# One-operation one-hot tables, a later choice for the fourth tile, and two-tile fronts in the first half of a decoder-layer kernel

## The chip, the cores and the metric

The kernel runs on one core of a Trainium2 chip. The metric is the device time of one execution in microseconds (us); less is better. The kernel before took 3437.81 us, the median of three runs (3435.53 to 3441.62). Its engines are TensorE (PE, with its weight loads as PEld), VectorE (DVE), ScalarE (ACT), GpSimd (POOL), which here issues the gathers, and SyncE (SP), which issues the other transfers.

## The reference

One decoder layer over 1024 tokens of width 1024, in float32. First a mixer (a gated short convolution and three groups of dilated attention, merged by sigmoid gates), then an expert layer:

```
s  = q . sub_keys                       # per token: 8 heads x 2 halves x 128 scores
top 16 of each half; top 16 of the 16x16 sums -> idx (of 16384 experts), gates = softmax
a  = gelu(x . expert_down[idx])         # 128 experts per token
h += sum_e gates_e * a_e * expert_up[idx_e]
out = rms_norm(h, final_norm)
```

## The kernel before

The tokens are worked on in two halves of 512, each of four tiles of 128 tokens. `mixer(0)` runs for the first half, then `mixer(1)` for the second. Every product with float32 weights is split: `weights` (L161) loads 512 KB, ScalarE rounds it to `hi` (L165), VectorE subtracts to get `lo` (L167), and `mm3` (L175 to L178) makes three matmuls per piece of 128 rows.

At the end of a mixer stand, for a *front* of tiles, the 16 gate projections (`gates`, L604), the merge (`merge`, L616: 8 projections of half depth with `w_attn_out`, 8 with `w_conv_out`), and for a *sub* of a front the output product (`product`, L663) and the `tail` (L694: norm, turn, 16 query projections of which the scores are stored). `SUBS` (L42) gives fronts and subs per half: `((1, 2), (1, 1))`, that is one front of four tiles with two subs of two tiles in the first half, and one of each in the second. While a tail waits at its start, `AFTER` = 4 steps of what comes next are put ahead of it.

The expert layer is done in two ways.

- **First half, by gathers** (`experts`, L872). For each of the four tiles `choose` (L756, VectorE alone, 16 rounds of top-8 operations and a decoding) gives 128 expert numbers per token. Each is a gather of 512 KB issued on POOL's queue into one of four row buffers: a *down* (L885 with the VectorE operation L887) or an *up* (L908 with L910). The steps are in the order of `STEPS` (L49): downs of tiles 0, 1, 2; ups of tile 0, which TensorE sums (`summed`, L930); ups of tiles 1 and 2; downs and ups of tile 3. Tile 0 is chosen during its own tail, tiles 1 to 3 in `mixer(1)` at the places that `CHOOSE = (0, 1, 2, 3)` (L47) gives: tile 3 during the second half's merge, and what is left of it at the start of `chosen(0)` (L1001).
- **Second half, densely** (`dense`, L971). TensorE multiplies all 16384 experts' down rows with the tokens (`hidden`, L985, 128 projections). The gates of the chosen experts become a dense table. `build` (L1011) makes for four tokens at a time (a *group*; 128 groups in all) two one-hot tables `oa` and `ob`, `ob` with the gate in it; TensorE multiplies them; ScalarE copies the product (`psg`) from PSUM into `stg`, which goes to memory (`g_d`) chunk by chunk, eight groups to a chunk. Then `weigh` (L1046) reads the whole table back expert by expert and multiplies, and TensorE applies the up rows.

`hidden` for the first ten blocks of four projections is interleaved with the four choices and builds of the second half and with `summed`; this is called the *hidden stretch* below. The first `weigh` needs every chunk of the table; from there on the kernel is in its *last stage*.

Before, `ob` is made in one of two ways: in every other group ScalarE takes four operations of 128 columns (L1029) and one of 512 (L1030) and VectorE one of 512 (L1031); in the others VectorE takes one of 512 (L1033) and ScalarE four of 128 (L1036). The copies are four of 128 columns (L1040).

A scheduler orders each engine's instructions when the program is built, from the order in which the code emits them (paced by `RATE_G` and the `PACE` constants) and from when buffers come free. The engines then run them in that fixed order.

## Time and profile before

| | us |
|---|---|
| median of three runs | 3437.81 |
| the profiled execution | 3448.45 |
| its span, first to last instruction | 3446.7 |
| TensorE busy | 3165.5 (92%) |
| VectorE busy | 2669.4 (77%) |
| ScalarE busy | 1398.0 (41%) |
| POOL busy | 1422.7 (41%) |

The profiled execution lies 10.6 us above the median of the runs. Times below are from the span's start. The stages: attention and gates of the first half until 650, its tails until about 790; `mixer(1)` until about 1500; its tail until 1620; the hidden stretch and the build until 2176; the last stage from 2198 on. A matmul's listed duration is longer than what it occupies, since matmuls are pipelined, and so, less strongly, is an operation's on VectorE and ScalarE: the time from one start to the next is the better measure where an engine doesn't wait.

### The profile page before, as it was taken

Reading aid. Unit: us, or ns where it says so; the run is one execution under the profiler, and the core shown is the slowest. Engines: PE = TensorE matmul, PEld = TensorE weight load, DVE = VectorE, ACT = ScalarE, POOL = GpSimd, SP = SyncE. Lnnn points to the kernel's source line nnn. Section 1 sums busy time; section 2 is a strip of 40 time slices with the busy share of each in tenths; the row PEclk is TensorE's granted clock in tenths of the full one; section 3 lists DMA queues with packets and bytes.
Section 4 is the critical chain, followed back from the end, with each engine's and each line's share of the span. In section 5 each row is a group of like instructions: output and inputs, shape, how many; then the busy total and the mean of one; then the engine's idle time right before and its main releaser. Section 6 shows DMA issues by size and latency. Waiting matters only on the chain.

```text
span 3446.7 us, 45451 instructions
## 1 busy us (share of the span) xinstructions
PE 3165.5 (92%) x15410; PEld 2559.9 (74%) x15410; DVE 2669.4 (77%) x5357; ACT 1398.0 (41%) x2898; POOL 1422.7 (41%) x1101
## 2 busy tenths in 40 slices
PE   7999999999899997979779985699999999999996
PEld 6788788887677875768556764588887878778775
DVE  5333455799999989888987748888887878778887
ACT  3544444543344362333465678332322232222222
POOL 0000000024555455555555334455555656555555
PEclk9999999999999997989889997799999999999998
DMA  4233345778888888999888887999999999999997
GB/s 131 77 118 115 95 136 201 237 251 308 295 297 306 306 304 276 344 321 338 307 295 328 322 316 280 335 341 329 324 347 327 333 330 329 327 322 336 322 318 276
DMA packets 349225, 965.26 MB, mean 280 GB/s; under 512 B 35264, under 2 KB 118720, under 8 KB 346432
## 3 DMA queue, kind: packets, MB, share of 16 engines
q0 software_dynamic: 152064, 551.62, 44.6%
q1 hardware_dynamic: 196928, 410.74, 35.0%
q8 instruction: 121, 1.98, 0.2%
q14 instruction: 112, 0.92, 0.1%
HBM read 885.61 MB, written 70.32 MB: 277 GB/s over the span
## 4 chain that ended last, share of the span: by engine, by line
PE 29%; DMA 16%; issue 14%; DVE 12%; POOL 9%; ACT 2%; SPq 1%; POOLq 0%; DVEq 0%; ACTq 0%
DMA rowu<-in_up,idx 7%; POOL row L885 6%; PE ps L178 5%; PE ps L176 5%; PE ps L177 5%; DMA row<-in_down,idx 4%; DVE row L887 4%; POOL rowu L908 3%; PE held L176 2%; PE held L177 2%; PE held L178 2%; PE psg L1038 2%; DVE lo L167 1%; PE upacc L944 1%; DVE acc L910 1%
## 5 line engine op out<-in xcount | busy, mean ns | idle before, releaser
L885 POOL DMA_INDIRECT row<-in_down,idx x512 | 668.9, 1306 | 670.9 <-DVE a L887 331.2
L908 POOL DMA_INDIRECT rowu<-in_up,idx x384 | 559.1, 1456 | 456.9 <-DVE acc L910 392.8
L165 ACT CAST hi<-raw 128x1024 fp32r<-128x1024 f32 x368 | 387.0, 1052 | 788.3 <-PE ps L177 491.7
L887 DVE CUSTOM_DVE_ANT_0 row<-row,ut 128x1024 f32<-128x1024 f32 x512 | 618.1, 1216 | 94.9 <-DMA row<-in_down,idx 89.3
L167 DVE TENSOR_TENSOR lo<-raw,hi 128x1024 fp32r<-128x1024 f32 x368 | 449.0, 1220 | 259.7 <-ACT hi L165 246.8
L910 DVE SCALAR_TENSOR_TENSOR acc<-rowu,a,acc 128x1024 f32<-128x1024 f32 x384 | 492.4, 1282 | 141.6 <-DMA rowu<-in_up,idx 132.1
L178 PE MATMUL ps<-vhi,lo 128*128 128x512 f32 (+1 forms) x1408 | 531.4, 377 | 29.1 <-DVE lo L167 27.4
L176 PE MATMUL ps<-vhi,hi 128*128 128x512 f32 (+1 forms) x1408 | 527.3, 375 | 5.8 <-ACT ga L989 3.6
L177 PE MATMUL ps<-vlo,hi 128*128 128x512 f32 (+1 forms) x1408 | 526.7, 374 | 0.1
L176 PE MATMUL ps<-uhi,hi 128*128 128x512 f32 x1024 | 407.0, 399 | 7.8 <-ACT hi L165 5.3
L178 PE MATMUL ps<-uhi,lo 128*128 128x512 f32 x1024 | 407.7, 399 | 2.0 <-DVE lo L167 1.9
L177 PE MATMUL ps<-ulo,hi 128*128 128x512 f32 x1024 | 406.7, 397 | 0.5 <-DVE ulo L182 0.5
L178 PEld LDWEIGHTS ps<-vhi,lo 128*128 128x128 f32 x1408 | 267.9, 190 | 84.5 <-DVE lo L167 34.7
L176 PE MATMUL held<-uh,hh 128*128 128x512 f32 x752 | 290.2, 395 | 24.9 <-ACT hh L181 24.9
L176 PEld LDWEIGHTS ps<-vhi,hi 128*128 128x128 f32 x1408 | 268.0, 190 | 54.8 <-ACT ga L989 5.3
L177 PEld LDWEIGHTS ps<-vlo,hi 128*128 128x128 f32 x1408 | 268.1, 190 | 46.7 <-issue 1.2
L177 PE MATMUL held<-ul,hh 128*128 128x512 f32 x752 | 297.1, 395 | 5.3 <-DVE ul L182 5.3
L178 PE MATMUL held<-uh,hl 128*128 128x512 f32 x752 | 294.9, 393 | 0.0
L181 ACT CAST uh<-rawu 128x1024 fp32r<-128x1024 f32 x126 | 131.6, 1049 | 380.6 <-DMA rawu<-in_up_s 310.8
L932 POOL DMA_DIRECT2D acc<-h_d x1 | 0.7, 691 | 619.1 <-DMA h_d<-h 619.1
L176 PEld LDWEIGHTS ps<-uhi,hi 128*128 128x128 f32 x1024 | 193.3, 189 | 54.5 <-ACT hi L165 7.8
L1038 PE MATMUL psg<-oa,ob 128*128 128x128 f32 x1024 | 157.9, 316 | 80.0 <-ACT stg L1040 42.7
(336 smaller groups left out, 5581.2 us busy)
## 6 DMA issues: line engine op xcount, KB each, us to landing
raw<-in_w_proj SPq DMA_DIRECT2D x128, 512.0 KB
raw<-in_down_t SPq DMA_DIRECT2D x128, 512.0 KB
rawu<-in_up_s SPq DMA_DIRECT2D x128, 512.0 KB
g_d<-stg SPq DMA_DIRECT2D x64, 512.0 KB
gg<-g_d SPq DMA_DIRECT2D x32, 1024.0 KB
raw<-in_w_query SPq DMA_DIRECT2D x48, 512.0 KB
raw<-in_w_v SPq DMA_DIRECT2D x24, 512.0 KB
raw<-in_w_out SPq DMA_DIRECT2D x24, 512.0 KB
```

The lines of the kernel that those rows point to most:

```text
L165: S.copy(hi, raw)
L167: V.tensor_tensor(lo, raw, hi.bitcast(F32), op=ALU.subtract)
L176: PE.matmul(ps, l[0], r[0], start=first, stop=False)
L177: PE.matmul(ps, l[0], r[1], start=False, stop=False)
L178: PE.matmul(ps, l[1], r[0], start=False, stop=last)
L181: S.copy(hi, src)
L885: G.indirect_dma_start(out=row, out_offset=None, in_=down, in_offset=bass.IndirectOffsetOnAxis(ap=idx[:, e:e + 1], axis=0))
L887: V.tensor_tensor_reduce(out=row, in0=row, in1=ut, scale=1.0, scalar=0.0, op0=ALU.mult, op1=ALU.add, accum_out=a[:, e:e + 1])
L908: G.indirect_dma_start(out=row, out_offset=None, in_=up, in_offset=bass.IndirectOffsetOnAxis(ap=idx[:, e:e + 1], axis=0))
L910: V.scalar_tensor_tensor(acc, row, a[:, e:e + 1], acc, op0=ALU.mult, op1=ALU.add)
L944: m = PE.matmul(part[n][32 * j:32 * j + 32], z[:, j, c0:c0 + 32], rows[j][:, n * TH:n * TH + TH], start=s == 0, stop=s == 31)
L1038: PE.matmul(ps[:, t], ob[:, t], oa[:, t], start=True, stop=True)
```

## The change

- The one-hot table `ob` is made by VectorE alone, four operations of 128 columns that compare and multiply in one; ScalarE has no part in it. The copies are two of 256 columns in place of four of 128, and the stores two of 1 MB per chunk in place of four of 512 KB. `OBUF` goes from 4 to 3 and `STG` from 5 buffers of 4 KB per partition to 3 of 8 KB.
- The choice for tile 3 of the first half is no longer advanced in `mixer(1)` and not finished in `chosen(0)`; it is emitted with the ups of tile 2, a step after every fourth up, once the builds have been emitted.
- `SUBS` is `((2, 1), (1, 1))`: the first half has two fronts of two tiles, each with its gates, merge, product and tail. Gate and merge weights are loaded and split twice, and their matmuls have 256 columns in place of 512. The first tile is chosen in the first front's tail.

```
-SUBS = ((1, 2), (1, 1))
-OBUF = 4
+SUBS = ((2, 1), (1, 1))
+OBUF = 3
-CHOOSE = (0, 1, 2, 3)
+CHOOSE = (0, 1, 2, 0)
-STG = 5
+STG = 3
...
                     V.scalar_tensor_tensor(acc, row, a[:, e:e + 1], acc, op0=ALU.mult, op1=ALU.add)
+                    if tt == 2 and e % 4 == 3:
+                        while "built" not in place:
+                            yield 1.0
+                        next(later[3], None)
                     yield 1.0
...
         def chosen(tt):
-            if tt == 0:
-                yield from later[ORDER[3]]
...
-                    stg = [den.tile([P, 32, TC], F32, tag="stg", bufs=STG, name="stg") for _ in range(4)]
+                    stg = [den.tile([P, 64, TC], F32, tag="stg", bufs=STG, name="stg") for _ in range(2)]
...
-                        if t4 % 2 == 0:
-                            for t in range(4):
-                                S.activation(ob[:, t], iota, AF.Abs, bias=i2[:, t:t + 1], scale=-1.0)
-                            S.activation(ob, ob, AF.Relu, bias=ones[:, 0:1], scale=-1.0)
-                            V.tensor_tensor(ob, ob, gv[:, :, None].to_broadcast([P, 4, P]), op=ALU.mult)
-                        else:
-                            V.tensor_tensor(ob, iota[:, None, :].to_broadcast([P, 4, P]),
-                                            i2[:, :, None].to_broadcast([P, 4, P]), op=ALU.is_equal)
-                            for t in range(4):
-                                S.mul(ob[:, t], ob[:, t], gv[:, t:t + 1])
+                        for t in range(4):
+                            V.tensor_scalar(ob[:, t], iota, i2[:, t:t + 1], gv[:, t:t + 1], op0=ALU.is_equal, op1=ALU.mult)
...
-                        for w in range(4):
+                        for w in range(2):
                             S.copy(stg[w][:, :, t4 * 4:t4 * 4 + 4],
-                                   ps[:, :, 32 * w:32 * w + 32].rearrange("p t i -> p i t"))
+                                   ps[:, :, 64 * w:64 * w + 64].rearrange("p t i -> p i t"))
...
         for _ in builder:
             yield 0.0
+        place["built"] = True
```

Three places in the order of the instructions. In the kernel after, lines behind L911 are numbered anew: L1025 becomes L1027, the new table operation is L1030, the copy L1034, the last stage's final sum L1145.

First, VectorE in the first half's merge (`sg` is a gate tile, `mlo` the low part of the merged one, L167 the split of the next weights). Before:

```order
L649 TENSOR_TENSOR sg_3713<-sg_3713,ys 128x512
L650 TENSOR_TENSOR sg_3713<-sg_3713,sg_3440 128x512
L182 TENSOR_TENSOR mlo_4538<-sg_3713,mhi_4536 128x512
L167 TENSOR_TENSOR lo<-raw,hi 128x1024
L649 TENSOR_TENSOR sg_3713<-sg_3713,ys 128x512
```

After, in the second front's merge (`tv`, `ti` belong to the choice of the next tile, L887 is a down):

```order
L649 TENSOR_TENSOR sg_5868<-sg_5868,ys 128x256
L765 MAX tv<-sv 128x8
L766 MAX_INDEX ti<-tv,sv 128x8 x3
L887 ISA row,a<-row,ut 128x1024
L887 ISA a 128x1
L167 TENSOR_TENSOR lo<-raw,hi 128x1024
L649 TENSOR_TENSOR sg_5868<-sg_5868,ys 128x256
L650 TENSOR_TENSOR sg_5868<-sg_5868,sg_4701 128x256
```

Before, no down and no step of a later choice stands ahead of the merge's end; after, downs of tile 0 and a choice stand between the second front's operations.

Second, ScalarE in the hidden stretch (L165 is the rounding of the next weights, `ga` the Gelu of a hidden projection). Before:

```order
L1040 COPY stg<-psg 128x32x4 x4
L1030 ACTIVATE ob<-ob,ones 128x512
L1036 ACTIVATE ob<-ob,sT 128x128 x4
L165 CAST hi<-raw 128x1024
L989 ACTIVATE ga<-ps 128x512
L1040 COPY stg<-psg 128x32x4
L1029 ACTIVATE ob<-iota,sT 128x128 x4
```

After:

```order
L1034 COPY stg<-psg 128x64x4 x2
L165 CAST hi<-raw 128x1024
L993 ACTIVATE ga<-ps 128x512
L1034 COPY stg<-psg 128x64x4 x6
L165 CAST hi<-raw 128x1024
L993 ACTIVATE ga<-ps 128x512
```

The table operations are gone from this queue; they stand on VectorE, between `oa` and whatever else is due there:

```order
L1027 TENSOR_TENSOR oa<-iota,sT 128x512
L1030 TENSOR_SCALAR ob<-iota,sT 128x128 x4
L167 TENSOR_TENSOR lo<-raw,hi 128x1024
L814 TENSOR_TENSOR e_17037<-e_17037,wq 128x256
L763 MAX_INDEX ti<-tv,sv 128x8
```

Third, VectorE at the program's end (`sts`, `st` are the final norms' small operations, L855 the scaled outputs: `h1b` of the second half, `acc` of the first half's last tile). Before:

```order
L910 SCALAR_TENSOR_TENSOR acc<-rowu,a,acc 128x1024
L206 TENSOR_TENSOR sts<-sts 128x1
L205 TENSOR_SCALAR sts<-sts 128x1
L203 TENSOR_TENSOR sts<-sts 128x1
L855 SCALAR_TENSOR_TENSOR h1b_27516<-h1b_27516,sts,nfin 128x512 x2
```

After:

```order
L206 TENSOR_TENSOR sts<-sts 128x1
L910 SCALAR_TENSOR_TENSOR acc<-rowu,a,acc 128x1024
L855 SCALAR_TENSOR_TENSOR h1b_27989<-h1b_27989,sts,nfin 128x512 x2
L910 SCALAR_TENSOR_TENSOR acc<-rowu,a,acc 128x1024 x21
L200 TENSOR_SCALAR st<-st 128x1
L202 RECIPROCAL st<-st 128x1
```

Before, the last up stands ahead of three of the second half's four scaled outputs; after, 21 ups stand behind the last of them.

## Rows read from the trace of the kernel before

**Rows 1.** The page's span in 40 equal slices, busy tenths of two engines.
```profile
PE   7999999999899997979779985699999999999996
DVE  5333455799999989888987748888887878778887
```

**Rows 2.** Stages: us, then PE, PEld, DVE, ACT, POOL busy (count), PEclk, DMA, GB/s.
```profile
441.00:650.00 209.00, 205.16 (x924) 166.93 (x923) 123.28 (x176) 98.69 (x144) 1.24 (x2) 1.00 0.57 193
650.00:750.00 100.00, 95.24 (x671) 88.75 (x670) 86.51 (x308) 47.22 (x98) 5.68 (x6) 0.95 0.62 194
750.00:1276.00 526.00, 504.92 (x2735) 412.82 (x2733) 502.92 (x1487) 230.16 (x433) 264.33 (x227) 0.98 0.89 307
1276.00:1620.00 344.00, 296.92 (x1287) 234.10 (x1286) 302.93 (x576) 111.14 (x181) 184.05 (x145) 0.90 0.90 318
1620.00:2018.00 398.00, 341.86 (x1919) 261.43 (x1921) 332.49 (x1149) 241.02 (x750) 191.61 (x168) 0.94 0.87 317
2018.00:2198.00 180.00, 100.28 (x610) 81.43 (x602) 121.97 (x158) 124.91 (x474) 84.17 (x67) 0.78 0.82 293
2198.00:3427.00 1229.00, 1198.52 (x5184) 978.15 (x5184) 1010.12 (x1032) 348.12 (x397) 686.79 (x475) 0.99 0.92 328
```

**Rows 3.** ScalarE's groups from 2018 to 2176: count | busy us, mean ns | idle before.
```profile
L1040 ACT COPY stg<-psg 128x128 f32<-128x128 f32 x224 | 45.5, 302 | 29.7 <-PE psg L1038 12.0 <-DMA g_d<-stg 10.6 <-remote 6.7
L1036 ACT ACTIVATE ob<-ob,sT 128x128 f32<-128x128 f32 x104 | 34.4, 434 | 1.8 <-DVE ob L1033 1.8
L1029 ACT ACTIVATE ob<-iota,sT 128x128 f32<-128x128 f32 x104 | 34.1, 436 | 0.0
L1030 ACT ACTIVATE ob<-ob,ones 128x512 f32<-128x512 f32 x26 | 20.0, 775 | 0.0
```

**Rows 4.** Waits from 2018 to 2176: total us, times, longest.
```profile
PE psg L1038 <- ACT stg L1040: 33.9, 14, 6.7
```

**Rows 5.** VectorE in order of time, in the build: start, us, operation.
```profile
2104.19 0.68 DVE L1033 TENSOR_TENSOR ob<-iota,sT 128x512 f32<-128x512 f32 x1
2104.79 1.28 DVE L910 SCALAR_TENSOR_TENSOR acc<-rowu,a,acc 128x1024 f32<-128x1024 f32 x1
2105.99 0.68 DVE L1031 TENSOR_TENSOR ob<-ob,sT 128x512 f32<-128x512 f32 x1
```

**Rows 6.** VectorE's groups by shape from 0 to 40.
```profile
L167 DVE TENSOR_TENSOR lo<-raw,hi 128x1024 fp32r<-128x1024 f32 x4 | 4.9, 1225 | 4.2 <-ACT hi L165 4.1
...
L257 DVE TENSOR_SCALAR ang<-ang,rc 128x512 f32<-128x512 f32 x1 | 0.5, 483 | 0.0
...
L259 DVE TENSOR_SCALAR nn<-ang 128x512 f32<-128x512 f32 x1 | 0.4, 422 | 0.0
...
L108 DVE TENSOR_SCALAR band<-diff 128x128 f32<-128x128 f32 x1 | 0.2, 245 | 0.2 <-POOL diff L106 0.2
```

**Rows 7.** TensorE in order of time: in the gates, a first-half tail, the build.
```profile
449.15 0.39 PE L178 MATMUL ps<-uhi,lo 128*128 128x512 f32 x1
449.38 0.39 PE L176 MATMUL ps<-uhi,hi 128*128 128x512 f32 x1
...
661.30 0.28 PE L177 MATMUL ps<-vlo,hi 128*128 128x256 f32 x1
661.42 0.28 PE L178 MATMUL ps<-vhi,lo 128*128 128x256 f32 x1
...
2099.81 1.43 PE L1038 MATMUL psg<-oa,ob 128*128 128x128 f32 x11
```

**Rows 8.** Line L885, the downs' gathers: duration ns, first and last start.
```profile
L885 POOL DMA_INDIRECT row<-in_down,idx x512: 932/1144/2948, 744.5 to 3107.4; - x171
```

**Rows 9.** VectorE at the end, in order of time.
```profile
3426.12 0.68 DVE L1150 TENSOR_TENSOR h1b<-h1b,held 128x512 f32<-128x512 f32 x1
...
3429.10 1.29 DVE L910 SCALAR_TENSOR_TENSOR acc<-rowu,a,acc 128x1024 f32<-128x1024 f32 x1 [0.78 <-DMA rowu<-in_up,idx]
...
3433.71 1.26 DVE L910 SCALAR_TENSOR_TENSOR acc<-rowu,a,acc 128x1024 f32<-128x1024 f32 x1
```

More of the change, by code (lines that the diff above doesn't have):

```diff
@@ L1026, in build @@
                                         i1[:, :, None].to_broadcast([P, 4, P]), op=ALU.is_equal)
-                        if t4 % 2 == 0:
-                            for t in range(4):
-                                S.activation(ob[:, t], iota, AF.Abs, bias=i2[:, t:t + 1], scale=-1.0)
-                            S.activation(ob, ob, AF.Relu, bias=ones[:, 0:1], scale=-1.0)
-                            V.tensor_tensor(ob, ob, gv[:, :, None].to_broadcast([P, 4, P]), op=ALU.mult)
-                        else:
-                            V.tensor_tensor(ob, iota[:, None, :].to_broadcast([P, 4, P]),
-                                            i2[:, :, None].to_broadcast([P, 4, P]), op=ALU.is_equal)
-                            for t in range(4):
-                                S.mul(ob[:, t], ob[:, t], gv[:, t:t + 1])
+                        for t in range(4):
+                            V.tensor_scalar(ob[:, t], iota, i2[:, t:t + 1], gv[:, t:t + 1], op0=ALU.is_equal, op1=ALU.mult)
                         for t in range(4):
                             PE.matmul(ps[:, t], ob[:, t], oa[:, t], start=True, stop=True)
-                        for w in range(4):
+                        for w in range(2):
                             S.copy(stg[w][:, :, t4 * 4:t4 * 4 + 4],
-                                   ps[:, :, 32 * w:32 * w + 32].rearrange("p t i -> p i t"))
+                                   ps[:, :, 64 * w:64 * w + 64].rearrange("p t i -> p i t"))
                         yield 1.1
-                    for w in range(4):
-                        nc.sync.dma_start(g_d[c, :, 32 * w:32 * w + 32], stg[w])
+                    for w in range(2):
+                        nc.sync.dma_start(g_d[c, :, 64 * w:64 * w + 64], stg[w])
         def weigh(q):
```

## The prediction

> **What bounds the kernel now.** First the slices of the page [rows 1], for where TensorE isn't full: from 650 to 1700 it is nearly so while VectorE is full too, then come holes at 2050 to 2200, and from there on it is full to the end. The stage table [rows 2] says the same with numbers. In the last stage TensorE is busy 1198.5 of 1229 us: it sets the pace. From 750 to 1276 both are full (VectorE 502.9, TensorE 504.9 of 526), from 1276 to 1620 VectorE is (302.9 of 344) and TensorE waits here and there (296.9). From 2018 to 2198 nothing is full on the page, though the table's build is all that is left: TensorE 100 of 180 us. ScalarE's groups [rows 3] tell why: 52 groups of the build take 45.5 us for copies and 34.4 + 34.1 + 20.0 us for its part of the tables, 134 us of 158, in one queue, so that a copy stands behind the next tables; and TensorE's product waits for the copy's `stg` side, 33.9 us in 14 waits [rows 4]. So the hole is ScalarE's, and the table is what the change takes from it. The gathers are a third thread: from the first down at 744.5 [rows 8] to the last up at 3433.7 [rows 9] they go on without a break, and they end beside TensorE's last work, not behind it.
>
> **The front, two tiles at a time.** A 512-column matmul follows the next after 0.23 us, a 256-column one after 0.12 [rows 7]. Gates 384, merge 96 and 192: 672 matmuls become 1344, 672 x (2 x 0.12 - 0.23) = 7 us more on TensorE; I take 9, from the finer means. 24 weights of 512 KB and 8 of 256 KB are loaded and split again: 24 x 1.2 us [rows 6] and 8 of half that, some 34 us on VectorE and as much on ScalarE, in a stage where VectorE is busy 123.3 of 209 us and the DMA engines 0.57 [rows 2]; that cover is gone for what falls behind the first gather, which is counted next. Ahead of tile 0's choice TensorE has half the gates (384 x 0.23 = 88 becomes 46), half the merge (66 becomes 35), one product in place of two (44 becomes 22), and four gate steps (12): 198 becomes 115, 83 us less. Narrow matmuls need their weights twice as fast, so I take 75: the first gather at 670 in place of 744.5.
>
> That gains nothing by itself where VectorE is full. By the order of both programs, 345 downs stand ahead of the hidden stretch's first split before and 378 after. From the first down to there VectorE gains 33 downs (38 us), 24 splits of the second front (27) and its other operations (19), and loses the fourth choice (37, at VectorE's start-to-start times): 47 us on 775. The trace took 870 us from 750 to 1620 [rows 2]; 870 x 822/775 = 923 from 675 gives 1598. By the downs' own pace, 870/345 = 2.52 us each, 378 give 1628. I take the middle: the hidden stretch starts at **1610** (before: 1620). The bounds are these two, and 25 us more if gathers and narrow matmuls want more of memory than there is: a 512 KB weight per 24 x 0.12 = 2.9 us is 180 GB/s, a down per 2.5 us 208, together over the 337 to 318 GB/s of the full stages [rows 2].
>
> **The hidden stretch.** From 1620 to 2018 TensorE is busy 342 of 398 us [rows 2]. Of that 39 projections x 24 x 0.23 = 215 us and 77 groups x 8 matmuls x 0.115 (11 in 1.43 us, the last listed to its end) = 71 are sure work [rows 7]; the rest is the sums of tile 0 and time inside matmuls. VectorE's work hardly changes: 77 groups lose 77 x 0.60 us of `ob` and gain four table operations each; 33 downs are gone; some of the fourth choice comes in, since the scheduler puts it here and not among the ups of tile 2. What does the new operation cost? None like it is in the trace. 128 columns without a per-partition number take 0.245 us, and such a number adds 0.061 at 512 columns (0.483 against 0.422) [rows 6]; this one has two: 0.31 to 0.37, and 0.23 to 0.29 from start to start, since VectorE's operations overlap by 0.08 (listed 0.68, next start 0.60) [rows 5]. I take 0.25, so 1.6 us for a group in place of 1.2, 51 us for all 128 groups. ScalarE loses its 1.7 us per group (88.5 us for 52) [rows 3], some 130 us for 77. Between the sure work, 286, and no change, 398, I take **350**, near TensorE's busy time: the cause in ScalarE's queue is gone, VectorE stays at the 0.83 it had. The stretch ends at 1960 (before: 2018).
>
> A rule speaks against this very operation. POOL's gathers are issued meanwhile, one in 1.14 us by the median and never over 2.95 [rows 8], and the trace has no stretch full of one-input VectorE operations to compare. The Trainium skill, "SBUF — State Buffer", section "Who interferes with whom", has it that a VectorE operation in a two-port mode, which a compare against per-partition numbers on float32 can use, locks GpSimd out of a shared port for its whole length, so that gathers can't write their descriptors. No run here shows it yet.
>
> **The end of the build.** Behind the stretch's last split the order has 51 groups left in both programs. Before they took 158 us, ScalarE's 134 among them. After, ScalarE has two copies of 256 columns per group, each between one and two times 0.30 us [rows 3]: 31 to 61 us. VectorE has 51 x 1.6 = 82 us, 9 ups at 1.2 [rows 5] and some 20 us of the fourth choice: 113, the new bound; at 0.9 busy 125 us. So the build ends at 1960 + 125 = 2085 (before 2176), and with the 22 us that store and first load take, the last stage starts at **2107** (before 2198): 91 us earlier.
>
> **The last stage and its end.** TensorE's work is the same, and VectorE's too by the order (475 gathered rows in place of 467 between first weigh and last sum): 1229 us again, 3336. But the gathers come later against it: 16 ups stand ahead of the first weigh where 41 did, and 21 stand behind the last sum, where 3 do [rows 9]. They go on at four buffers' pace, 2.3 us each in the last rows (3429.10 to 3433.71 for two) [rows 9]; I take 2.2: 46 us, to 3382, and 13 us for the last norm, store and end as now (3433.7 to 3446.7). Span 3395, **52 us less**. On the profiled execution that is 3448.45 - 52 = 3396; the median of the runs lies 10.6 below it: **3385**.
>
> **The rivals.**
>
> *VectorE takes ScalarE's place.* The build is a pipeline of three engines, and 0.4 us per group go to the one that is full before and after it. If the hidden stretch stays 398 us and the end of the build 158, the last stage starts at 1610 + 398 + 158 + 22 = 2188, and 21 trailing ups cost 39 us more than 3 do now: 3476 of span, slower: 3467 for the median. It decides from a last stage that starts later than 2159. For it: VectorE is the only engine that is at 0.83 in this stretch. Against: TensorE's waits name `stg`, and no VectorE operation for long [rows 4].
>
> *The gain is only partly there:* the stretch takes 385 us, the end 140, which is 3445 of span, 3436, and no change.
>
> *More than that.* TensorE alone sets the stretch (325 us), the build ends 110 us later, the ups trail at POOL's pace of 1.14 us [rows 8], 24 us in all: 3333 of span, 3324.
>
> *The front costs.* Gathers and narrow matmuls share memory; the hidden stretch starts 35 us later: 3420.
>
> *The lock of the port:* each of some 128 gathers in the stretch waits for up to four table operations, 0.9 us, if it meets them; they fill a fifth of the time. 23 us of stretch if all of it is felt: 3408. The rule that bears on it is the one named above.
>
> That the fourth choice doesn't move to the ups of tile 2 is no rival but in the sum: the order has it at the build's end.
>
> **How the numbers follow.** Chances: the forecast 0.48 (3350 to 3425 for its own bounds: 0.23 and 0.29 us per operation, 330 and 375 us of stretch, 1.8 to 2.5 us per trailing up); more 0.17; the front costs 0.08; the lock 0.03; partly 0.09; VectorE in ScalarE's place 0.15. Within 0.2% (7 us, about what a measurement of this kernel can tell from no change) is the partial case alone, 0.09; slower 0.15; faster 0.76. The range goes from inside the better case to beyond the partial one, 3310 to 3455, and leaves out the slow rival and the far end of the good one.
>
> **What would show it.** The first down at about 670. ScalarE's time per group of the build under 1.3 us, and TensorE's waits for `stg` gone. The new operation near 0.33 us listed. TensorE's hole ahead of the first weigh 30 us shorter or more, the first weigh near 2107. 21 ups behind the last sum, in 40 to 50 us. I am wrong if the first weigh comes after 2159, if the last stage is longer than 1229 us by more than 15, or if POOL's issues grow in the stretch.

## The result and the profile after

The changed kernel takes 3457.65 us in the median of seven runs (3449.58 to 3470.2), the kernel before 3437.97 beside it: a ratio of 1.0052, 95% interval 1.0033 to 1.0071. It is slower, where 1.5% faster was forecast. Below, "after" is its profiled execution, 3470.2 us with a span of 3468.4.

First the two rows of the page that answer to [rows 1]:

```profile
PE   7999989977999999889999985999999999999991
DVE  4333476999998888988899899888788887788887
```

TensorE's hole ahead of the last stage is one slice at 5 (5 and 6 before), with VectorE at 9 in it, and another has come at the end: in the last slice TensorE is done (1) and VectorE isn't (7). The stages, with the columns of [rows 2], cut where their boundaries now lie (first down, last attention stages, first and last split of the hidden stretch, 2 us short of the build's last copy, first weigh to last sum, what trails):

```profile
441.00:692.00 251.00, 231.96 (x1719) 219.35 (x1719) 193.80 (x470) 138.04 (x242) 7.93 (x8) 0.97 0.64 218
692.00:1276.00 584.00, 539.73 (x2962) 443.19 (x2961) 530.82 (x1353) 238.40 (x455) 292.07 (x240) 0.96 0.91 318
1276.00:1650.00 374.00, 343.15 (x1582) 276.82 (x1583) 323.99 (x605) 130.63 (x218) 204.27 (x157) 0.95 0.91 323
1650.00:2009.00 359.00, 353.51 (x1986) 254.97 (x1985) 328.01 (x1357) 126.34 (x269) 155.31 (x153) 1.00 0.86 325
2009.00:2133.00 124.00, 92.49 (x542) 78.59 (x541) 121.47 (x434) 40.16 (x117) 29.37 (x27) 0.81 0.60 219
2152.00:3398.00 1246.00, 1203.74 (x5184) 978.73 (x5184) 1016.48 (x1052) 347.02 (x395) 712.99 (x474) 0.99 0.91 324
3398.00:3468.00 70.00, 0.00 (x0) 0.00 (x0) 46.01 (x65) 2.48 (x7) 38.11 (x29) 0.50 0.74 252
```

The hidden stretch is 359 us (398 before) with TensorE busy 353.5, and the build's end, to the last copy, 126 (158 before). The forecast put this down to the table; how much of it is the table's is taken up again below. The row 2009:2133 says what it cost: VectorE busy 121.5 of 124 us, the DMA engines 0.60, 219 GB/s. Before, from 2018 to 2176, these were 108.7 of 158 us, 0.79 and 284:

```profile
2018.00:2176.00 158.00, 100.28 (x610) 81.43 (x602) 108.73 (x147) 121.03 (x470) 74.40 (x59) 0.82 0.79 284
```

The groups of 2009:2133 after (count | busy us, mean ns | idle before), which answer to [rows 3], and its longest wait of TensorE, which answers to [rows 4]:

```profile
L1030 DVE TENSOR_SCALAR ob<-iota,sT 128x128 f32<-128x128 f32 x204 | 56.3, 344 | 0.0
L1034 ACT COPY stg<-psg 128x256 f32<-128x256 f32 x106 | 34.7, 375 | 80.5 <-PE psg L1032 65.1 <-issue 7.4 <-DMA g_d<-stg 7.0
...
L908 POOL DMA_INDIRECT rowu<-in_up,idx x13 | 15.5, 1192 | 59.4 <-DVE acc L910 30.3 <-DVE bp L784 11.2 <-DVE e L783 6.1
L910 DVE SCALAR_TENSOR_TENSOR acc<-rowu,a,acc 128x1024 f32<-128x1024 f32 x10 | 12.8, 1275 | 0.0
```

```profile
PE psg L1032 <- DVE ob L1030: 26.8, 17, 5.5
```

ScalarE has only copies left and idles 80 us. TensorE waits for VectorE's table in place of ScalarE's copy (3.4 us are left of that wait). And POOL's gathers often stand still for VectorE, 59 us ahead of ups: 13 are issued and 10 summed in these 124 us. The end, VectorE in order of time (start, us), answers to [rows 9]:

```profile
3397.73 0.68 DVE L1145 TENSOR_TENSOR h1b<-h1b,held 128x512 f32<-128x512 f32 x1
3398.33 1.28 DVE L910 SCALAR_TENSOR_TENSOR acc<-rowu,a,acc 128x1024 f32<-128x1024 f32 x1
...
3458.08 1.28 DVE L910 SCALAR_TENSOR_TENSOR acc<-rowu,a,acc 128x1024 f32<-128x1024 f32 x1 [0.80 <-DMA rowu<-in_up,idx]
```

Behind the last sum of TensorE's work 29 ups trail for 60 us (before, 4 for 8 us). Two threads run through this kernel, and it ends with the later of them. Their marks, each a start on VectorE or TensorE read from the two traces:

| us | before | after | |
|---|---|---|---|
| first down | 749.9 | 692.4 | -57 |
| hidden stretch, first split | 1620.4 | 1650.3 | +30 |
| 384th down | 1747.9 | 1663.0 | -85 |
| first up | 2088.6 | 2075.3 | -13 |
| 33rd up | 2174.2 | 2210.9 | +37 |
| first weigh | 2197.8 | 2152.3 | -46 |
| TensorE's last matmul | 3419.2 | 3391.0 | **-28** |
| last up | 3433.7 | 3458.1 | **+24** |

TensorE's thread did gain, 28 us. The gathers' thread lost 24, and as the two ended 15 us apart before, the loss is what counts. (The profiled execution after is the slowest of the seven; in another of the same kernel, e9 below, the last two marks are 3388 and 3454.)

Of the lead of 85 us at the 384th down 13 are left at the first up. Between these two POOL issues the 128 summed rows, and in the same queue the loads of scores (`sv`) for the choices, into two buffers. POOL's rows from the one mark to the other, before and then after:

```profile
L958 POOL DMA_INDIRECT rowu<-in_up,iT x62 | 72.5, 1170 | 136.9 <-PE upacc L944 118.1 <-issue 11.9 <-DMA rowb<-in_up,iT 3.6
L839 POOL DMA_DIRECT2D sv<-s_d x15 | 8.9, 592 | 12.6 <-DVE ti L766 5.8 <-DVE dec L801 3.2 <-DVE sv L764 2.2
```

```profile
L962 POOL DMA_INDIRECT rowu<-in_up,iT x62 | 68.6, 1106 | 105.9 <-PE upacc L948 85.1 <-issue 7.0 <-PE psg L1032 5.9
L839 POOL DMA_DIRECT2D sv<-s_d x30 | 17.7, 591 | 80.5 <-DVE ti L766 40.3 <-DVE ti L763 19.7 <-DVE tv L765 8.5
```

POOL waits for TensorE's sums less than before, 85 us in place of 118. What grew is the idle time ahead of the `sv` loads, which wait for VectorE's choices: 12.6 us became 80.5, about as much as the 72 us of lead that were lost. In part these are loads that stood ahead of the 384th down before; counted from the start of the hidden stretch they are 22 with 18.1 us before and 30 with 80.5 after. So the gathers lost to VectorE here too. No run changes these waits alone.

### The profile page after: what moved, and what is told of

Read it like the earlier page. It is cut to its first block, busy times and chain, and to the rows that moved or that the text cites. A ratio compares the mean times of both kernels' runs of the same rounds, so it can differ in the third digit from the quotient of the medians.

```text
span 3468.4 us, 46567 instructions
## 1 busy us (share of the span) xinstructions
PE 3186.9 (92%) x16082; PEld 2588.3 (75%) x16082; DVE 2755.1 (79%) x5805; ACT 1223.9 (35%) x2130; POOL 1450.2 (42%) x1101
## 3 DMA queue, kind: packets, MB, share of 16 engines
q8 instruction: 127, 2.08, 0.2%
## 4 chain that ended last, share of the span: by engine, by line
PE 24%; DMA 18%; issue 16%; POOL 12%; DVE 12%; ACT 1%; POOLq 0%; SPq 0%; DVEq 0%; ACTq 0%
DMA rowu<-in_up,idx 11%; POOL row L885 8%; PE ps L178 5%; PE ps L176 5%; PE ps L177 5%; POOL rowu L908 4%; DMA row<-in_down,idx 4%; PE psg L1032 2%; DVE row L887 2%; PE upacc L948 2%; DVE acc L910 2%; DVE lo L167 2%; DVE ob L1030 1%; PE sc L467 1%; DMA rowu<-in_up,iT 1%
## 5 line engine op out<-in xcount | busy, mean ns | idle before, releaser
L885 POOL DMA_INDIRECT row<-in_down,idx x512 | 684.3, 1336 | 658.4 <-DVE a L887 392.4
L908 POOL DMA_INDIRECT rowu<-in_up,idx x384 | 580.3, 1511 | 485.9 <-DVE acc L910 366.4
L887 DVE CUSTOM_DVE_ANT_0 row<-row,ut 128x1024 f32<-128x1024 f32 x512 | 618.8, 1219 | 155.1 <-DMA row<-in_down,idx 149.7
L165 ACT CAST hi<-raw 128x1024 fp32r<-128x1024 f32 x392 | 411.7, 1050 | 856.7 <-PE ps L177 620.0
L167 DVE TENSOR_TENSOR lo<-raw,hi 128x1024 fp32r<-128x1024 f32 x392 | 477.9, 1219 | 215.8 <-ACT hi L165 204.5
L910 DVE SCALAR_TENSOR_TENSOR acc<-rowu,a,acc 128x1024 f32<-128x1024 f32 x384 | 492.2, 1282 | 167.6 <-DMA rowu<-in_up,idx 155.7
L178 PE MATMUL ps<-uhi,lo 128*128 128x512 f32 (+1 forms) x1152 | 434.2, 377 | 13.4 <-DVE lo L167 13.4
L176 PE MATMUL ps<-uhi,hi 128*128 128x512 f32 (+1 forms) x1152 | 432.9, 377 | 10.5 <-ACT hi L165 7.6
L177 PE MATMUL ps<-ulo,hi 128*128 128x512 f32 (+1 forms) x1152 | 431.5, 375 | 0.6 <-DVE ulo L182 0.5
L178 PEld LDWEIGHTS ps<-uhi,lo 128*128 128x128 f32 x1152 | 220.6, 192 | 56.7 <-DVE lo L167 18.9
L176 PEld LDWEIGHTS ps<-uhi,hi 128*128 128x128 f32 x1152 | 221.0, 192 | 51.4 <-ACT hi L165 9.4
L177 PEld LDWEIGHTS ps<-ulo,hi 128*128 128x128 f32 x1152 | 221.0, 192 | 39.4 <-issue 2.3
```

Source lines behind the costliest of these rows:

```text
L165: S.copy(hi, raw)
L167: V.tensor_tensor(lo, raw, hi.bitcast(F32), op=ALU.subtract)
L176: PE.matmul(ps, l[0], r[0], start=first, stop=False)
L177: PE.matmul(ps, l[0], r[1], start=False, stop=False)
L178: PE.matmul(ps, l[1], r[0], start=False, stop=last)
L885: G.indirect_dma_start(out=row, out_offset=None, in_=down, in_offset=bass.IndirectOffsetOnAxis(ap=idx[:, e:e + 1], axis=0))
```

## The experiments

Times are medians; each ratio is to the kernel before on the same chip, with its 95% interval. The marks are of each profiled execution.

| run | what it is | us, ratio | first weigh | TensorE's end | last up |
|---|---|---|---|---|---|
| e1_table | before + table | 3477.3, 1.0076 (1.0057 to 1.0094) | 2166 | 3392 | 3471 |
| e2_nofront | after, whole front | 3483.9, 1.0107 (1.0083 to 1.0131) | 2149 | 3374 | 3461 |
| e3_nolater | after, fourth choice early | 3467.6, 1.0055 (1.0034 to 1.0076) | 2164 | 3388 | 3453 |
| e4_front | before + split front | 3458.0, 1.0018 (1.0003 to 1.0033) | 2219 | 3445 | 3424 |
| e5_nogate | after, no gates in the table | 3435.2, 0.9966 (0.995 to 0.9982) | 2144 | 3364 | 3421 |
| e6_rows5 | after + fifth row buffer | 3428.4, 0.9952 (0.9932 to 0.9972) | 2153 | 3349 | 3414 |
| e7_extra | after + 16.8 MB of loads | 3516.9, 1.02 (1.0159 to 1.0242) | 2203 | 3422 | 3509 |
| e8_mixed | after, new form in half the groups | 3435.1, 0.997 (0.9949 to 0.9991) | 2154 | 3372 | 3428 |
| e9_again | after | 3465.1, 1.0043 (1.0022 to 1.0063) | 2161 | 3388 | 3454 |
| e10_wide | after, old second table | 3455.4, 1.0014 (0.9991 to 1.0037) | 2223 | 3437 | 3395 |
| e11_ups6 | after, six weight buffers | 3459.1, 1.0026 (1.0004 to 1.0048) | 2172 | 3388 | 3450 |
| e12_both | e8 + e6 | 3406.8, 0.9874 (0.984 to 0.9907) | 2145 | 3334 | 3400 |
| e13_noload | after, second front loads nothing | 3468.5, 1.0106 (1.0073 to 1.0138) | 2185 | 3411 | 3467 |
| e14_nosplit | after, second front without low parts | 3460.5, 1.0073 (1.0046 to 1.01) | 2164 | 3388 | 3452 |
| e16_rows5b | before + fifth row buffer | 3436.5, 1.0003 (0.9987 to 1.0018) | 2178 | 3367 | 3433 |
| e17_best | after, compare + gates on ScalarE, fifth buffer | 3412.0, 0.9928 (0.9905 to 0.9952) | 2147 | 3336 | 3402 |
| e18_late | e17, fifth buffer taken up later | 3390.0, 0.9833 (0.9817 to 0.9849) | 2172 | 3361 | 3389 |
| e19_late_b | before + fifth buffer taken up later | 3409.8, 0.9896 (0.9877 to 0.9914) | 2184 | 3374 | 3398 |

**Which part lost it.** Three theories: the gathers' thread sets the end (G), the split front lost the time (F), the later choice did (L). The edits are whole parts of the change, done alone (e1, e4) or undone (e2, e3):

```diff
 e1_table, against before: all of the table's lines, for the two forms of ob
+for t in range(4):
+    V.tensor_scalar(ob[:, t], iota, i2[:, t:t + 1], gv[:, t:t + 1], op0=ALU.is_equal, op1=ALU.mult)
...
 e3_nolater, against after
-CHOOSE = (0, 1, 2, 0)
+CHOOSE = (0, 1, 2, 3)
+            if tt == 0:
+                yield from later[ORDER[3]]
 e2_nofront, against after
-SUBS = ((2, 1), (1, 1))
+SUBS = ((1, 2), (1, 1))
 e4_front, against before
-SUBS = ((1, 2), (1, 1))
+SUBS = ((2, 1), (1, 1))
```

> The kernel before with the new table alone (one operation per token's table, two 256-column copies, buffers as in the changed kernel). Theory G: the end is set by the gathers, a thread of 1024 transfers without a break that shares memory with the loads of weights; it starts at 744 and ends near 3434 as before, whatever TensorE does, and more of it trails behind TensorE: first weigh some 70 us earlier than 2198, TensorE done 50 us or more before the end, time within 10 us of the kernel before (ratio 1.000, 0.997 to 1.006). Theory F: the split front alone lost the time, the table gains what was predicted: first weigh at 2115, time 50 to 80 us less (ratio 0.978 to 0.985). Theory L: the later choice lost it, so the table alone gains too, 0.985.

> The changed kernel with the front of the first half whole again (four tiles at a time): the new table and the later choice alone. Theory G: first gather at 744 again and 15 MB less to move (965 in place of 980 MB, 47 us at the 319 GB/s that the kernel before moved from its first gather to its last); the gathers starve at the end of the build as in the changed kernel, some 20 to 35 us: ratio to the kernel before 1.003 to 1.010, about the changed kernel's 1.005. Theory F: with the front gone the gain of the table is there, ratio 0.978 to 0.985. Theory L: worse than the changed kernel by what the front gave, 1.010 or more.

> The changed kernel with the fourth tile's choice where the kernel before has it: the new table and the split front alone. Theory G: the gathers start at 690, move 980 MB, and starve less behind the hidden stretch since the choice is done; ratio 0.995 to 1.003. Theory F: as slow as the changed kernel, 1.003 to 1.008. Theory L: the loss is gone, and the table's gain shows: 0.980 to 0.990.

> The kernel before with the split front alone. Theory G: the gathers start 55 to 60 us earlier and 15 MB more have to be moved, 47 us at 319 GB/s: ratio 0.995 to 1.000, and TensorE is what ends last, since the order has no up behind the last sum. Theory F: the second front runs under a full VectorE, and the hidden stretch starts 35 to 80 us later; nothing else gives it back: ratio 1.010 to 1.023. Theory L: no loss, 0.985 to 1.000.

F and L fall with e1: the table alone, which both put at 0.985 or less, is slower, and by no less than the whole change (1.0057 to 1.0094, against 1.0033 to 1.0071). G's ranges were missed too: all four runs came out slower than them (1.006, 1.010, 1.003 and 1.000 at most), e2 where L had it and e3 where F had it. What speaks for G are the marks. In e1 the two threads part already, as the stage rows of e1 from its first weigh to TensorE's end and behind it show:

```profile
2166.00:3392.00 1226.00, 1200.86 (x5184) 978.53 (x5184) 999.96 (x1014) 345.07 (x389) 700.58 (x468) 0.99 0.92 327
3392.00:3472.00 80.00, 0.25 (x2) 0.00 (x0) 57.80 (x78) 3.81 (x11) 48.37 (x37) 0.52 0.83 277
```

First weigh 32 us earlier, a last stage as long as before, TensorE done at 3392 (3419), and then 80 us of ups alone. The split front is worth some 0.2 to 0.6% together with the table (e1 to e3, e2 to after) and costs 0.2% without it: it moves the gathers forward and TensorE back (e4 ends with TensorE, at 3445). The later choice costs 0.3% by the medians of e1 and e2, whose intervals overlap, and with the split front, e3 to after, nothing that can be told.

These runs also say what shortened the hidden stretch. First e1, the table alone, then e10 (below), which has the old table with the split front and the later choice, each from first to last split:

```profile
1628.00:2045.00 417.00, 371.16 (x2022) 277.85 (x2022) 371.83 (x1405) 131.35 (x284) 187.55 (x173) 0.93 0.85 313
```

```profile
1653.00:2003.00 350.00, 337.77 (x1896) 245.83 (x1894) 297.22 (x1190) 212.25 (x534) 178.59 (x155) 0.99 0.87 323
```

With the table alone the stretch is 417 us, longer than the 398 before; with the old table it is 350, as short as the 358 after. The table shortens the stretch and the build's end together, from first split to last copy: by 38 us alone (556 before, 518 in e1), by 65 behind the other two parts (549 in e10, 485 after).

**What of the table costs.** Theory V: the new operation takes VectorE from the ups. Rival M: memory sets the gathers' pace whatever VectorE does. e5 gives VectorE back all of it by leaving the gates out, e8 half, e10 all of it by the old two forms, which ScalarE shares:

```diff
 e5_nogate
-for t in range(4):
-    V.tensor_scalar(ob[:, t], iota, i2[:, t:t + 1], gv[:, t:t + 1], op0=ALU.is_equal, op1=ALU.mult)
+V.tensor_tensor(ob, iota[:, None, :].to_broadcast([P, 4, P]),
+                i2[:, :, None].to_broadcast([P, 4, P]), op=ALU.is_equal)
 e8_mixed: the new form where t4 % 2 == 0, else
+V.tensor_tensor(ob, iota[:, None, :].to_broadcast([P, 4, P]),
+                i2[:, :, None].to_broadcast([P, 4, P]), op=ALU.is_equal)
+for t in range(4):
+    S.mul(ob[:, t], ob[:, t], gv[:, t:t + 1])
 e10_wide: the second table's lines of the kernel before
-    V.tensor_scalar(ob[:, t], iota, i2[:, t:t + 1], gv[:, t:t + 1], op0=ALU.is_equal, op1=ALU.mult)
+if t4 % 2 == 0:
+    for t in range(4):
+        S.activation(ob[:, t], iota, AF.Abs, bias=i2[:, t:t + 1], scale=-1.0)
...
```

> The changed kernel, with the gates left out of the table (its second table is one compare over four tokens, 0.60 us on VectorE in place of 4 x 0.256; ScalarE has no part of it), so that VectorE's work per group is the 1.2 us of the kernel before. Theory V: the new operation takes VectorE from the gathers' own sums (ups) in the build, and that is what the table costs: with 0.42 us per group gone (54 us of VectorE), the first weigh comes 20 to 40 us before 2152, the up sums start sooner, and the last up ends 25 to 45 us before 3458; ratio to the kernel before 0.993 to 0.998. Theory M: memory sets the gathers' pace from the first to the last, whatever VectorE does: the last up ends within 10 us of 3458, ratio 1.003 to 1.006, and only TensorE's end moves.

> The changed kernel with the new operation in every second group of the table only; the others have the kernel before's form (one compare of 0.60 us on VectorE and four multiplications on ScalarE). Theory V: VectorE has 1.4 us per group in place of 1.62, 27 us less, ScalarE 1.2 us in place of 0.54, still off the path: the last up ends 10 to 25 us earlier, ratio 0.998 to 1.002. Theory M: no change, 1.003 to 1.007.

> The changed kernel once more, beside the next three on one chip, since the runs of e5 to e8 have been set against the kernel before only. If the ratio of 1.0052 holds (1.003 to 1.007), the gains of e5, e6 and e8 against it stand, 0.8 to 1.0 per cent each. If it comes out at 0.996 to 0.999, this chip moves the changed kernel as a whole, and e5, e6 and e8 showed nothing.

> The changed kernel with the kernel before's two forms of the second table, so that of the table's change only the two wide copies per group are left (with the split front and the later choice). VectorE has 1.2 us per group again, ScalarE some 2.3 us. Theory V: VectorE's share of the table is what the gathers lose; the ups run at 2.6 us in the build's end as in the kernel before (65 of them stand ahead of the first weigh by the order), the first weigh comes late (2180 to 2220) and TensorE is the last again: ratio 0.996 to 1.003. Theory M: as the changed kernel, 1.003 to 1.007.

e9 sets the base: the changed kernel is slower by the same in another comparison. Against it, each by its ratio to the kernel before, e5 is 0.8% faster and e8 0.7%, so V holds: of the 54 us of VectorE that e5 takes away (128 groups x 0.42) the kernel gets 27 to 32 back, by the ratios and by the profiled executions. e8, which takes 27 us away, gets nearly as much; why the other 27 bring so little more stays open. The ups say where, by VectorE's rows of L910 from the first up on (count, duration, first and last start), first e9, then e8:

```profile
L910 DVE SCALAR_TENSOR_TENSOR acc<-rowu,a,acc x33: 1222/1275/1319, 2084.8 to 2218.0; 128x1024 f32<-128x1024 f32 x33
```

```profile
L910 DVE SCALAR_TENSOR_TENSOR acc<-rowu,a,acc x43: 1277/1285/1320, 2074.1 to 2217.7; 128x1024 f32<-128x1024 f32 x43
```

By 2218 the one has summed 33 rows, the other 43. The first weigh moved by 7 us alone (in e5 by 8 from 2152, where 20 to 40 were expected). So the price was not paid in the table's own time, where I had looked for it, but by the thread that shares VectorE. e10 is the other side of it: with the old forms 65 ups stand ahead of the first weigh by the order and TensorE ends last again, 3437; the first weigh comes later than in the kernel before. The wide copies and the fewer buffers, with the split front and the later choice, bring nothing that can be told; no run has `OBUF` or `STG` changed alone.

**Whether memory or the row buffers set the last stage.** e6 puts a fifth row buffer in the room of a weight buffer, e11 takes that weight buffer away alone, e7 adds loads:

```diff
 e6_rows5
-UPS = 7
+UPS = 6
+        spare.extend([ctx.enter_context(tc.tile_pool(name="more", bufs=1))] * 1)
 e11_ups6
-UPS = 7
+UPS = 6
 e7_extra
+                    nc.sync.dma_start(extra, up_s[(NB * q + ii) // 2, n, :, 0, 0:256])
```

> The changed kernel with a fifth buffer for gathered rows from the first weigh on (and six in place of seven buffers for the split weights, whose room it takes). Theory B: the last stage's gathers run at the pace of four buffers, each held for about 10.5 us (7 us from issue to landing, then the wait for VectorE and its 1.28 us), so 2.63 us per row; a fifth gives 2.2 to 2.4 us, some 490 rows gain 100 us or more of their thread until TensorE is the last again (3391 and its 35 us more): ratio 0.985 to 0.995. Theory M: memory is full (326 GB/s and a DMA share of 0.91 in the stage), more transfers in flight only land later: the pace stays 2.55 to 2.65, ratio 1.002 to 1.008.

> The changed kernel with six in place of seven buffers for the split weights of the last stage, which e6 needed for its fifth row buffer. Expected within 0.2 per cent of the changed kernel beside it (e9), so that e6's gain is the fifth buffer's. If it is itself 0.5 per cent faster, e6's gain was not the buffer's.

> The changed kernel with 128 loads of 128 KB added in the last stage, one behind each load of its weights, into a buffer that nothing reads: 16.8 MB more. Theory M: memory sets the pace, so the end comes later by 16.8 MB at the stage's 326 GB/s, 51 us: ratio to the kernel before 1.017 to 1.022. Theory B: the gathers wait for their own four buffers, the extra loads fit into the room that is left: 0 to 15 us, ratio 1.005 to 1.010.

> The mixed table of e8 with the fifth row buffer of e6. If the two gains are of different stages (e8's 30 us before and in the build's end, e6's 30 us in the last stage, where a row then takes 2.52 in place of 2.65 us), they add up: 55 us under the changed kernel, ratio to the kernel before 0.988 to 0.991. If both only take room from the same limit, 0.994 to 0.997.

The buffers have part of it. From first weigh to TensorE's end, e9 and then e6:

```profile
2160.00:3388.00 1228.00, 1200.61 (x5184) 978.36 (x5184) 1010.11 (x1038) 342.38 (x387) 708.52 (x472) 0.99 0.92 327
```

```profile
2153.00:3349.00 1196.00, 1188.13 (x5183) 975.73 (x5184) 1017.35 (x1042) 350.42 (x396) 665.25 (x477) 1.00 0.94 338
```

327 GB/s become 338, a row in the stage goes from 2.64 to 2.54 us and a trailing one from 2.05 to 1.73: memory had room, as B says, but a row was to take 2.2 to 2.4 us, so four buffers are not all that holds it. TensorE's stage is 32 us shorter too; I take it that rows which come late hold VectorE's queue and the splits behind them, but no run isolates that. e11 lies within the uncertainty of e9 (0.17% by the medians), so the gain is the row buffer's. The gains of e8 and e6 add up in e12, 1.7% under e9. e7 came out at M's number for another reason, and decides nothing: the scheduler had put 91 of the 128 loads ahead of the first weigh. SyncE's queue in order of time (start, us, count):

```profile
2131.67 0.90 SPq L1038 DMA_DIRECT2D g_d<-stg  x2
2135.65 22.84 SPq L1118 DMA_DIRECT2D extra<-in_up_s  x9
2158.55 0.90 SPq L1038 DMA_DIRECT2D g_d<-stg  x2
```

Up to nine loads into the one buffer, one behind the other, stand ahead of a pair of the table's stores, and the first weigh came 43 us after e9's. Its last stage, with the other 37, was no longer than e9's (1219 us).

**What holds the second front.** In every run with the split front the hidden stretch starts at 1650 or later, where I had 1610. Open were the loads (M) and VectorE's splits (V):

```diff
 e13_noload: weights() of the second front's gates and of its eight large merge weights
-raw = wp.tile([P, n, D // n], F32, tag="raw", bufs=RAWS, name="raw")
-nc.sync.dma_start(raw, src)
+raw = qp.rearrange("p a b -> p (a b)")[:, 0:D].rearrange("p (n k) -> p n k", n=n)
 e14_nosplit: the same weights
-V.tensor_tensor(lo, raw, hi.bitcast(F32), op=ALU.subtract)
-return hi, lo
+return hi, hi
```

> The changed kernel, whose second front does not load its 24 large weights again (16 of the gates, 8 of the merge) but splits what stands in the queries' buffer of the attention, so its values are not the layer's: 12.6 MB of loads gone, every split and matmul kept. Theory M: the second loads are what holds the hidden stretch back (first gelu at 1660 in place of the 1610 predicted): 12.6 MB at the 318 GB/s of the stage are 40 us, first gelu at 1615 to 1630, time 25 to 45 us less than the changed kernel. Theory V: the second front is held by VectorE, which has downs, choices and splits in one queue: first gelu at 1650 to 1665, time within 12 us of the changed kernel.

> The changed kernel, whose second front loads its 24 large weights but leaves out their low part on VectorE (the high part stands in its place in the products, so its values are not the layer's): 24 x 1.22 = 29 us of VectorE gone in the second front, loads and matmuls kept. Theory V: VectorE sets that stage, first gelu 25 to 35 us before 1660, time 20 to 35 us less than the changed kernel. Theory M: within 10 us of 1660 and of the changed kernel.

Neither moved it forward. Without 12.6 MB of loads the stretch starts at 1671, without 29 us of VectorE at 1659 (by first splits; after 1650, e9 1651). But these runs take little from the stage itself: 18 of the 24 weights are split ahead of the first down. There VectorE's splits seem to count: e14's first down comes at 672, after's at 692 (e13's at 698). Between first down and stretch only six of the splits, and at most six of the loads, are gone, and the order of both runs puts six more downs there. VectorE from 692 to 920, e9, e13 and e14:

```profile
692.00:920.00 228.00, 186.80 (x1044) 160.06 (x1043) 220.11 (x604) 79.72 (x129) 102.99 (x92) 0.93 0.93 332
```

```profile
692.00:920.00 228.00, 180.08 (x1000) 155.29 (x1000) 213.84 (x586) 75.86 (x124) 105.55 (x92) 0.90 0.90 312
```

```profile
692.00:920.00 228.00, 199.56 (x1141) 173.34 (x1141) 217.44 (x619) 86.69 (x139) 93.54 (x88) 0.94 0.94 339
```

VectorE stays as full, and TensorE is busy 180 to 200 us of 228 each time. What agrees better is simpler: the order puts a fixed number of downs ahead of the stretch's first split, and they come at nearly one pace. Time from first down to that split, divided by the downs between: before 345 in 871 us, 2.52; e2 341, 2.50; e1 345, 2.53; after 378 in 958, 2.53; e13 384, 2.53; e14 384, 2.57; e4 371, 2.61; e3 371, 2.61. (From 2.50 to 2.61 are still 40 us on 378 rows.) What sets 2.5 us a row there isn't settled: e13 and e14 rule out neither memory nor VectorE, and no run has a fifth buffer this early.

**Whether the order holds the rest.** e16 is the kernel before with e6's buffer, e17 the changed one with that and a third form of the table; e18 is e17, and e19 is e16, with the buffer in use two blocks later:

```diff
 e17_best, every group
+V.tensor_tensor(ob, iota[:, None, :].to_broadcast([P, 4, P]),
+                i2[:, :, None].to_broadcast([P, 4, P]), op=ALU.is_equal)
+for t in range(4):
+    S.mul(ob[:, t], ob[:, t], gv[:, t:t + 1])
 e18_late, e19_late_b
+        more = ctx.enter_context(tc.tile_pool(name="more", bufs=1))
...
+            if n_q == 2:
+                spare.append(more)
```

> The kernel before with the fifth row buffer from the first weigh on (and six buffers for split weights). In e6 it gave the changed kernel 0.9 per cent: the last stage went from 1228 to 1196 us, a row from 2.64 to 2.52 us. Theory B: it is the buffers that set the gathers' pace in the last stage of both kernels, and here TensorE and the gathers end together, so both gain: ratio 0.988 to 0.993. Rival: here TensorE is the last by itself, and fewer buffers for its weights cost it: 0.998 to 1.003.

> The changed kernel with every second table as one compare over four tokens on VectorE (0.60 us) and four multiplications by the gate on ScalarE, and the fifth row buffer: VectorE has 1.2 us per group as in the kernel before, ScalarE some 1.85 us in place of 2.6. Theory V: VectorE is what the gathers lack in the build; against e12 (1.41 us per group) another 27 us of VectorE are gone, and ScalarE's 51 x 1.85 = 94 us of the build's end stay under the 105 us it takes: the last up 8 to 20 us earlier than in e12, ratio 0.982 to 0.986. Rival: ScalarE is the bound of the build's end again, first weigh at 2170 or later, ratio 0.987 to 0.993.

> The kernel of e17 with the fifth row buffer taken into use only from the third block of the last stage on. In e6, e12, e16 and e17 it lies in memory that the build gives back, so that the order lets only four ups start ahead of the first weigh and leaves 37 behind the last sum, whatever VectorE has free; here the order has 29 ahead and 15 behind. Theory O (order): the ups that trail alone at 1.8 us a row come under TensorE's work: against e17 the last up 20 to 40 us earlier, TensorE's end up to 15 us later, ratio 5 to 12 thousandths under that of e17. Rival: the last stage takes the same rows at the pace that memory gives, and is longer by what trails less: within 3 thousandths of e17.

> The kernel before with the fifth row buffer in use from the third block of the last stage on. In e16 TensorE ended 52 us sooner with it and the gathers no sooner, since the order kept 37 rows for the end; here 29 ups stand ahead of the first weigh and 12 behind the last sum. Theory O: the gathers end 20 to 40 us earlier than 3433, ratio 0.988 to 0.994. Rival: first weigh and the stage are later by as much, ratio 0.997 to 1.002.

e16 gains nothing, though TensorE ends 52 us sooner, and e17's last up comes where e12's does (3402 and 3400; by its ratio e17 is no faster), though VectorE has 27 us less to do. Both ratios are those of the rivals, but not by their mechanisms: in e16 TensorE isn't the last, in e17 the first weigh isn't late (2147). Both have four ups ahead of the first weigh and 37 behind the last sum. POOL's waits of e17 from the first up to the first weigh (total us, times, longest) show the gap:

```profile
POOL rowu L908 <- issue: 47.7, 1, 47.7
```

and in order of time (start, us, idle before) the gather that ends it:

```profile
2140.34 0.94 POOL L908 DMA_INDIRECT rowu<-in_up,idx  x1 [47.70 <-issue]
```

This gather stands 47.7 us with no engine named, until 7 us behind the build's last copy (2133): the fifth buffer's pool is opened in memory that the build gives back, and the gathers queue behind the one that is to use it. Taken up later (29 ups ahead, 15 and 12 behind), the trail is short, and both ratios are where theory O had them. Of its marks e19's last up fits (35 us sooner), while in e18 the last up comes 13 us sooner than in e17, not 20 to 40, and TensorE's end 25 later, not up to 15. The stretch behind TensorE's end, e17 and then e18:

```profile
3336.00:3404.00 68.00, 0.59 (x3) 0.17 (x1) 55.44 (x68) 1.68 (x6) 46.78 (x36) 0.54 0.89 315
```

```profile
3361.00:3391.00 30.00, 0.69 (x4) 0.23 (x2) 27.16 (x48) 1.67 (x6) 16.85 (x14) 0.55 0.88 331
```

e18 at 3390.0 us beats both kernels, by 1.7% the one before. Beside e19 on the same chip it is 0.6% faster: that is what the split front, the later choice, the wide copies and a one-form table are worth once the row buffer is there.

## Why the prediction was wrong

**The table's operation was sized right, its gain only in part.** The new operation is listed at 344 ns (0.33 forecast) and starts every 0.256 us (0.25). ScalarE's copies are two of 375 ns, and TensorE's waits for `stg` are down from 33.9 to 3.4 us. The hidden stretch has 358 us from first to last split (350), the end of the build 126 (125), the step to the first weigh 17 (22). But I put all 81 us of stretch and build (556 to 475) down to the table, because "the cause in ScalarE's queue is gone". It brings 38 alone and 65 behind the other parts, and the old table behind them has a stretch of 350 us too (e10). That this term came out near is in good part luck.

**The chain lost 73 us elsewhere:** 40 at the start of the stretch, 8 in it, 1 in the build's end, 17 in the last stage, 14 in the ups that trail, less 7 in the step to the first weigh and behind the last up. Span 3395 became 3468.4.

*The front's term failed, +40.* The first down came at 692, not 675: the first choice began 62 us sooner than before (653 to 591), not 75. And for the stretch's start I took the middle of two figures, 1598 by VectorE's work and 1628 by the downs' own pace. The second came nearer: from 692.4, 378 downs at the 2.52 us of before give 1645, and it came at 1650. The first failed in its last step, 870 x 822/775, where the time was to grow as VectorE's work does. The work grew as I had it, from 806 to 855 us busy between first down and stretch; the time grew from 871 to 958, as VectorE's wait for the downs' rows went from 34.8 to 90.0 us. The rival "the front costs" had the size (35 us), by memory; e13, which takes few loads out of this stage, doesn't settle that cause. (The 337 GB/s beside it stands in no row of [rows 2], where the most is 328.)

*The trailing ups, +14.* I counted 21, the ups behind the last scaled output. Behind the last sum, from which I reckoned, are 29 (before 4, not 3), and from first weigh to last sum 467 rows, as before, not 475; at 2.08 us (2.2 forecast) they make 60 us, not 46. The decision point of 2159 was wrong with it: the first weigh came before it, at 2152, and the kernel is slower.

*The last stage, +17,* is partly this one execution's: in e9 it is 1234 us (2160.5 to 3394.3) where I had 1229. It is the one of my three signs of being wrong that was met.

**The deeper fault is that I made one chain of it.** I wrote that the gathers "end beside TensorE's last work", then gave them only a count of trailing rows. They are a chain with VectorE in it at every row. VectorE was called the new bound of the build's end, rightly, at 0.9 busy (it is 0.98), and then priced by the table's time alone. The first rival, VectorE in ScalarE's place, named the right engine at the wrong place: the stretch and the build did get shorter, and the loss was the gathers': 68 us more of waits ahead of the `sv` loads, and 50 in the first 33 ups, which took 136 us, 86 before. e5 and e8 show the table's time on VectorE as cause and not only as company: 0.7 to 0.8% come back when it is given back.

**The lock of the port** is not seen. By the rows of the summed gathers in the hidden stretch, where VectorE has some 300 of the new operation, POOL's issue is no slower than before. After, then before:

```profile
L962 POOL DMA_INDIRECT rowb<-in_up,iT x64 | 75.0, 1172 | 25.1 <-issue 15.8 <-DMA rowu<-in_up,iT 4.7 <-PE upacc L948 2.7
```

```profile
L958 POOL DMA_INDIRECT rowb<-in_up,iT x56 | 72.1, 1288 | 17.2 <-issue 15.5 <-DMA rowu<-in_up,iT 0.8 <-DMA rowb<-in_up,iT 0.3
```

The Trainium skill, "SBUF — State Buffer", section "Who interferes with whom", ties the lock to VectorE's two-port modes; the trace doesn't say in which mode this operation runs, so the rule isn't refuted, only not met here. No row of L885 in the whole run is over 2.21 us (2.95 before, [rows 8]).

**What could have warned before the run:** the last sum and the last up stand 8 us apart in [rows 9], so a step that helps TensorE and loads VectorE has to be followed down both threads. With 16 ups ahead of the first weigh in place of 41, which I had, 25 more rows come behind TensorE's work, 55 us at the 2.2 that I took. That alone would not have turned a first weigh 91 us earlier into a loss; against the 46 us by which it did come forward it does.

## What to carry to other kernels

Where two threads of work end together, sum a change for each of them; moving work from an engine that one of them waits for to the one that both pass through speeds the first thread and slows the other. In a queue that is issued in order, count what stands ahead of a mark and multiply by the pace of the slowest kind in it; freed time of the engine may move nothing while that count stays, as in e17. And ask of a new buffer whose memory it takes over, since that, and not its size, may decide when it can first be used.

## What the runs showed of the hardware

A compare and multiply against two per-partition numbers on 128 float32 columns takes 0.256 us on VectorE from start to start (344 ns listed), a compare alone over four tokens and 512 columns 0.60 (e5): four narrow operations cost 1.7 wide ones. With DMA engines at 0.92 and 327 GB/s a fifth gather in flight still brought 340 GB/s at 0.95 (e17, e18), and the rows that trail alone go from 2.05 us each (e9) to 1.76 and 1.79: a DMA share of 0.92 was not a full memory.
